# A hybrid decoder step on one core: values of the forgetting attention in a tile a head, the normalisation of a pair of heads taken up within the next pair, lasting zero-padded tiles for small inverses

## The chip, the core and the metric

The kernel runs on one core of a Trainium2 chip, as one launch. The time is the device time of that core in microseconds (us). The core has TensorE (PE), which does the matmuls and the transposes, VectorE (DVE), ScalarE (ACT), GpSimd (POOL), and SyncE (SP), whose queue issues most of the loads. Each engine takes its instructions in the order in which they were built in, and waits at the head of its queue for what that instruction needs. DMAs are issued from SP, ACT and POOL.

## The reference

One inference step with 1024 prompt tokens and 32 sample tokens. One input projection feeds four groups of heads; their outputs, each times a SiLU gate, are joined by an output projection and a layer norm. Two groups matter here:

```python
# C: forgetting attention (FoX), 8 heads x 64, blocks of 128 queries
s = einsum('bqhd,bkhd->bhqk', q, k) * 64 ** -0.5 + cq[.., :, None] - ck[.., None, :]   # cumulative log-forget
p = softmax(where(k_pos <= q_pos, s, -1e30));  o = einsum('bhqk,bkhd->bqhd', p, v)      # then times silu(c_gate)

# A: gated DeltaNet (GDN), 4 heads x 128, chunk-wise WY form, state S carried from chunk to chunk
sol = triangular_solve(eye + a, concat([v * beta, k * beta * exp(gam)]))               # per chunk
u = w_val - w_key @ S;  o = q_dec @ S + qk @ u;  S = S * chunk_dec + k_tail.T @ u
```

## The kernel before

The program runs in three stretches. First come the input projections, woven with the decoding of the sample tokens against the paged cache. The second, which the change touches, computes FoX and GDN for the prompt, woven with the last gate projections and with the cross-attention; the third does the SSD group, the output projection and the layer norm.

FoX takes its eight heads in pairs: `fox(hp)` does pair `hp`, heads `2*hp` and `2*hp + 1` (`h2` is 0 or 1). A head has four steps (`m`), each for two blocks of 128 queries. In a step PE computes logits into PSUM (`fs`, L588), DVE adds the forget term and takes the minimum (L592), ACT takes the exponential (L598), PE transposes the probabilities (`ft`), ACT or DVE copies them out (`P`), PE multiplies them with the values (`fo`, L620, whose weights are the tile `vt`), and DVE multiplies the result with the gate into `g2` (L626). The values of a pair are written to DRAM by `fox_v` in the first stretch as `vD[hp]`, 128 x 1024, and loaded into the one buffer of `vt` on SP's queue (L568), 512 KB. When both heads of a pair are done, the pair is normalised at once: DVE inverts the sums, ACT spreads them into `rr` (L636), PE transposes `rr` into the PSUM buffer that `ft` also uses (there is one), DVE multiplies into `g2` (L640), twice (`a`), and ACT's queue stores `g2`.

GDN takes 8 half-heads of four chunks (`i`). `gdn_solve` inverts the triangular matrices of half-head `i + 1` while `gdn_scan` carries the state through half-head `i`. The 16 x 16 inverses lie in DRAM (`dX`); `gdn_inv` clears a tile `D1` on DVE (L1039) and loads eight blocks into it (L1041, `D<-dX` in the trace). The matrices `A` have one buffer: the load for the next solve (L1057, `A<-aD`) waits until PE has done `l2p` (L1123), the last matmuls that read the old one. DVE reads the new one in `AL` (L1082).

The order on each engine is not written out by hand. Generators are woven (64 steps of FoX to 37 of GDN), and when the program is built a scheduler with a timeline of its own orders the instructions of each engine.

Of the kernel before, what the change touches and what calls it, by code (L numbers as in the profile page):

```python
# [21 lines left out]
T = 1024  # L22
# [148 lines left out]
class K:  # L171
# [356 lines left out]
    def fox_v(self, hp):  # L528
        nc, O = self.nc, self.O
        v = self.row_tile("vf")  # L530
        yield from self.projt(f"cv{hp}", lambda j, o, ps: self.copy(v[:, o:o + JW], ps))
        nc.scalar.dma_start(O["vT"][:, hp, :], v[:, :TT])
        vt = self.row_tile("vt")
        for a in range(2):
            p = self.g("vt")
            for b in range(4):
                n = 4 * a + b
                self.tr(p[:, b * 128:(b + 1) * 128], v[:, n * 128:(n + 1) * 128])
            self.copy(vt[:, 512 * a:512 * a + 512], p)
        nc.scalar.dma_start(self.vD[hp], vt[:, :T])  # L540
        p = self.g("vs")
        self.tr(p[:NS, 0:128], v[:, T:TT])
        nc.vector.tensor_copy(self.vs[:, hp * 128:(hp + 1) * 128], p[:NS, 0:128])

    def fox(self, hp):


        nc, fx = self.nc, self.fx
        vt = fx.tile([128, 8, 128], F32, tag="vt", name="vt", bufs=1)
        g2 = fx.tile([128, T], F32, tag="g2", name="g2", bufs=2)  # L550
# [5 lines left out]
        for h2 in range(2):  # L556
# [8 lines left out]
            self.marks.append(self.row(12 + hd, cB, nc.gpsimd))  # L565
            if h2 == 0:
                with behind(self.gl, hd - GL):
                    nc.sync.dma_start(vt, self.vD[hp].rearrange("p (n c) -> p n c", c=128))  # L568
                    nc.sync.dma_start(g2, self.gateD[8 + hp])
# [4 lines left out]
            for m in range(4):  # L574
                pair = (2 * m, 2 * m + 1)
                mns, Ss = {}, {}
                for qt in pair:
# [18 lines left out]
                    for i, (c0, c1) in enumerate(ch):  # L596
                        S, w = Ss[qt, i], c1 - c0
                        nc.scalar.activation(out=S[:, :w], in_=S[:, :w], func=AF.Exp, scale=-1.0, bias=mn[:, 0:1], accum_out=rs[:, qt, h2, i:i + 1])  # L598
                yield
                o = self.g("fo")  # L600
                for i in range(len(ch)):
# [11 lines left out]
                    for b4 in range(nb[pair[1]]):  # L613
                        kt = 4 * i + b4
                        for half in (1, 0):
                            qt = pair[half]
                            if b4 >= nb[qt]:
                                continue
                            with self.tc.issue_after(first.ins) if first else nullcontext():
                                d = nc.tensor.matmul(o[64 * half:64 * half + 64, 0:128], lhsT=vt[:, kt, 64 * h2:64 * h2 + 64],  # L620
                                                     rhs=P[qt, b4], start=(kt == 0), stop=(kt == qt), tile_position=(0, 64 * half))
                            first = first or d
                r = slice(64 * h2, 64 * h2 + 64)
                for half, qt in enumerate(pair):
                    s = slice(qt * 128, qt * 128 + 128)
                    nc.vector.tensor_tensor(out=g2[r, s], in0=o[64 * half:64 * half + 64, 0:128], in1=g2[r, s], op=ALU.mult)  # L626
                yield

        ri = fx.tile([128, 8, 2], F32, tag="ri", name="ri", bufs=2)
        nc.vector.tensor_tensor(out=ri, in0=rs[:, :, :, 0], in1=rs[:, :, :, 1], op=ALU.add)  # L630
        nc.vector.tensor_scalar(out=ri, in0=ri, scalar1=2.0, scalar2=None, op0=ALU.mult)
        nc.vector.reciprocal(ri, ri)
        for a in range(2):
# [6 lines left out]
            nc.vector.tensor_tensor(out=g2[:, s], in0=p, in1=g2[:, s], op=ALU.mult)  # L640
        nc.scalar.dma_start(self.mixD[2][:, hp, :], g2)

# [372 lines left out]
    def gdn(self):  # L1015


        w = {}

        self.scan = self.g("su")  # L1020
        self.gdn_inv(0)
        run(self.gdn_solve(0, w))
        self.gdn_loads(0)
        for i in range(8):
            nxt = {}
            solve = self.gdn_solve(i + 1, nxt) if i < 7 else iter(())
            for n, _ in enumerate(self.gdn_scan(i, w)):
                next(solve, None), next(solve, None)
                if n == 1 and i < 7:
                    self.gdn_loads(i + 1)  # L1030
                yield
            run(solve)
            w = nxt

    def gdn_inv(self, i):

        nc, (h, a), N = self.nc, divmod(i, 2), 4
        D1 = self.ga.tile([128, N, 32], F32, tag="D1", name="D1", bufs=2)
        nc.vector.memset(D1, 0.0)  # L1039
        for b in range(8):  # L1040
# [19 lines left out]
    def gdn_solve(self, i, w):  # L1060
# [13 lines left out]

        D1, DT1, AL, P1, P3 = self.D1[i], sm("DT1"), sm("AL"), sm("P1", 16), sm("P3")
        A, DT = big("A", D["A"], eng), big("DT")
        nc.vector.memset(DT, 0.0)
        if i < 7:
            self.gdn_inv(i + 1)
        nc.vector.transpose(out=fl(DT1), in_=fl(D1))  # L1080
        for q in Q:
# [8 lines left out]
        for n in range(N):  # L1090
            for i, q in enumerate(Q):
                nc.tensor.matmul(p[q, n * 16:(n + 1) * 16], lhsT=D1[q, n, :], rhs=P1[q, n, :], start=True, stop=True, tile_position=(32 * i, 32 * i))
        nc.vector.tensor_tensor(out=DT1[:, :, 16:32], in0=DT1[:, :, 16:32], in1=p[:, 0:N * 16].rearrange("p (n c) -> p n c", n=N), op=ALU.subtract)
# [542 lines left out]
    def run(self):  # L1636
# [4 lines left out]
        with ExitStack() as self.ctx_x:  # L1641
# [50 lines left out]

            def foxes():
                for hp in range(4):
                    yield from self.fox(hp)

# [112 lines left out]
```

## Time and profile before

| | |
|---|---|
| median of 3 runs | 1435.81 us (1434.82 to 1438.54) |
| the profiled execution | 1434.86 us, of which 1433.1 from its first to its last instruction |
| PE busy | 1329.7 us, 93% |
| DVE, ACT, POOL busy | 57%, 35%, 31% |
| granted TensorE clock, mean | 0.976 |

PE is nearly always busy, so what counts is when it stands still, what ended each such gap, and where its clock is below 1.00. Time in which another engine is idle counts only where PE waits behind it.

### The profile page before, as it was taken

To read this page: it belongs to the slowest core of one execution; us is meant where nothing else is said; L and a number is where in the kernel's file an instruction comes from. 1 tells how busy PE (TensorE), PEld (TensorE's weight loads), DVE (VectorE), ACT (ScalarE), POOL (GpSimd) and SP (SyncE) were. 2 spreads that over 40 slices of the span, in tenths; PEclk is the share of its full clock that TensorE was granted. 3 is DMA by queue.
4 is the path that set the end of the run, shared out by engine and by line. 5 is a ranking of instruction groups with operands and counts; after the bars stand their busy time and mean duration, and the time that the engine had idled before them with its cause. 6 is when DMAs were issued, how large, how long until landed. Compare 5 with 4: busy or idle time off the path is not lost. (4 is left out here: it accounts for less than half of the span.)

```text
span 1433.1 us, 30270 instructions
## 1 busy us (share of the span) xinstructions
PE 1329.7 (93%) x11222; PEld 1110.0 (77%) x11222; DVE 823.8 (57%) x2141; ACT 494.7 (35%) x1280; POOL 442.4 (31%) x465
## 2 busy tenths in 40 slices
PE   7999999999899999999998899898988979999995
PEld 6899888888778877888887878776766756666764
DVE  4523223256576767534245655677676648856588
ACT  4422222233435343322233244454444421213232
POOL 1445322233425444432212100011111026544456
PEclk9999999999999999999999999899999999999998
DMA  6559888978778897888877834657547576655322
GB/s 246 196 169 374 331 299 323 321 269 281 240 284 306 282 307 248 303 287 323 308 259 175 239 91 118 239 147 208 137 129 252 175 234 205 198 160 121 96 67 106
DMA packets 184477, 324.30 MB, mean 226 GB/s; under 512 B 47177, under 2 KB 110954, under 8 KB 184330
## 3 DMA queue, kind: packets, MB, share of 16 engines
q1 hardware_dynamic: 113744, 241.39, 50.4%
q10 hardware_dynamic: 41930, 59.11, 11.6%
q0 software_dynamic: 28656, 21.88, 6.2%
q8 instruction: 88, 1.44, 0.4%
q14 instruction: 59, 0.48, 0.1%
HBM read 262.23 MB, written 60.01 MB: 225 GB/s over the span
## 5 line engine op out<-in xcount | busy, mean ns | idle before, releaser
L356 PE MATMUL pj<-xh,wh 128*128 128x352 f32 x1152 | 382.2, 333 | 13.1 <-ACT wh L341 5.0
L356 PE MATMUL pj<-xh,wl 128*128 128x352 f32 x1152 | 379.5, 329 | 3.3 <-DVE wl L342 3.3
L356 PE MATMUL pj<-xl,wh 128*128 128x352 f32 x1152 | 379.1, 329 | 0.0
L356 PEld LDWEIGHTS pj<-xh,wh 128*128 128x128 f32 x1152 | 219.1, 191 | 28.1 <-issue 10.7
L356 PEld LDWEIGHTS pj<-xh,wl 128*128 128x128 f32 x1152 | 219.8, 191 | 11.5 <-issue 6.3
L356 PEld LDWEIGHTS pj<-xl,wh 128*128 128x128 f32 x1152 | 219.3, 190 | 10.6 <-issue 9.9
L1574 PE MATMUL op<-wo,mh 128*128 128x512 f32 x512 | 162.9, 398 | 3.1 <-DVE lr L1587 1.6
L672 POOL DMA_INDIRECT lf<-in_logf,ix x64 | 67.9, 1062 | 203.4 <-DVE cb L675 163.4
L342 POOL TENSOR_TENSOR wl<-wr,wh 128x1024 fp32r<-128x1024 f32 x41 | 97.9, 2387 | 104.3 <-ACT wh L341 94.3
L742 DVE SCALAR_TENSOR_TENSOR Oacc<-Oacc,dmb,dO 128x512 f32<-128x512 f32 x64 | 47.5, 743 | 142.3 <-PE dO L737 134.1
L1574 PEld LDWEIGHTS op<-wo,mh 128*128 128x128 f32 x512 | 95.6, 190 | 29.6 <-issue 6.0
L1574 PE MATMUL op<-wo,ml 128*128 128x512 f32 x256 | 102.0, 401 | 5.5 <-POOL ml L1546 5.5
L917 DVE SCALAR_TENSOR_TENSOR y<-u,cw,y 128x1080 f32<-128x1080 f32 x54 | 80.1, 1484 | 21.9 <-ACT y L915 21.5
L718 PEld LDWEIGHTS dA<-pg,QD 128*32 128x32 f32 x2048 | 59.8, 109 | 39.7 <-issue 25.8
L718 PE MATMUL dA<-pg,QD 128*32 128x128 f32 x2048 | 80.6, 275 | 7.6 <-DMA pg<-in_cache 7.5
L598 ACT ACTIVATE S<-S,mn 128x512 f32<-128x512 f32 (+2 forms) x96 | 58.5, 610 | 50.8 <-DVE mn L592 24.3
L737 PE MATMUL dO<-pg,dP 128*32 128x512 f32 x512 | 71.8, 605 | 4.1 <-ACT dP L734 3.9
L726 ACT ACTIVATE dmb<-dmb 128x1 f32<-128x1 f32 x64 | 18.7, 293 | 131.6 <-DVE dmb L725 116.3
L1574 PEld LDWEIGHTS op<-wo,ml 128*128 128x128 f32 x256 | 48.4, 189 | 20.2 <-POOL ml L1546 7.1
L592 DVE CUSTOM_DVE_ANT_0 S<-fs,cB 128x512 f32<-128x512 f32 (+2 forms) x96 | 52.5, 551 | 19.9 <-PE ft L219 15.0
L1193 POOL TENSOR_TENSOR rb<-ra,constG 128x4 f32<-128x4 f32 (+1 forms) x9 | 8.7, 971 | 156.5 <-DVE ra L1192 156.5
L620 PE MATMUL fo<-P,vt 128*64 128x128 f32 x576 | 47.9, 288 | 9.6 <-DMA vt<-vD 7.7
(521 smaller groups left out, 2450.2 us busy)
## 6 DMA issues: line engine op xcount, KB each, us to landing
pg<-in_cache SPq DMA_DIRECT2D x256, 512.0 KB
wr<-in_w_in SPq DMA_DIRECT2D x48, 512.0 KB
k<-kD POOLq DMA_DIRECT2D x16, 512.0 KB, 18.2
wq<-in_w_out SPq DMA_DIRECT2D x16, 512.0 KB
mr<-mixD SPq DMA_DIRECT2D x32, 256.0 KB
xr<-in_xT SPq DMA_DIRECT2D x8, 528.0 KB
gateD<-gt ACTq DMA_DIRECT2D x24, 176.0 KB
mrow<-in_w_mem SPq DMA_DIRECT2D x8, 512.0 KB
```

The costliest lines, as they stand in the source:

```text
L342: (eng or self.se).tensor_tensor(out=l, in0=r, in1=h.bitcast(F32), op=ALU.subtract)
L356: nc.tensor.matmul(ps[:n], lhsT=w[:, k, :], rhs=x[:, k, s], start=(k == 0 and q == 0), stop=(k == KD - 1 and q == 2))
L592: nc.vector.tensor_tensor_reduce(out=S[:, :w], in0=p[:, :w], in1=cB[:, c0:c1], op0=ALU.add, op1=ALU.min, scale=1.0, scalar=3e38, accum_out ...
L598: nc.scalar.activation(out=S[:, :w], in_=S[:, :w], func=AF.Exp, scale=-1.0, bias=mn[:, 0:1], accum_out=rs[:, qt, h2, i:i + 1])
L620: d = nc.tensor.matmul(o[64 * half:64 * half + 64, 0:128], lhsT=vt[:, kt, 64 * h2:64 * h2 + 64], rhs=P[qt, b4], start=(kt == 0), stop=(kt ...
L672: nc.gpsimd.indirect_dma_start(out=lf, out_offset=None, in_=I["logf"], in_offset=bass.IndirectOffsetOnAxis(ap=ix[:, j:j + 1].bitcast(U32), ...
L718: nc.tensor.matmul(ps[32 * b:32 * b + 32, 0:n], lhsT=QD[:, 4 * gr + b, hp, :], rhs=key(hp, b), start=(hp == 0), stop=(hp == 3), tile_posit ...
L726: nc.scalar.activation(out=mb[:, 1:2], in_=m, func=AF.Exp, scale=-1.0, bias=mb[:, 0:1])
L737: nc.tensor.matmul(po[32 * b:32 * b + 32, :], lhsT=P[:n, 32 * b:32 * b + 32], rhs=value(b), start=True, stop=True, tile_position=(0, 32 * b))
L742: nc.vector.scalar_tensor_tensor(out=O_, in0=O_, scalar=mb[:, 1:2], in1=po, op0=ALU.mult, op1=ALU.add)
L917: nc.vector.scalar_tensor_tensor(out=y, in0=u[:, i:i + CWD], scalar=w[:, i:i + 1], in1=y, op0=ALU.mult, op1=ALU.add)
L1574: nc.tensor.matmul(p[:m], lhsT=l[:, k, :], rhs=W[k][0][:, w, s], start=(k == 0 and q == 0), stop=(k == kn - 1 and q == 2))
```

## The change

- `fox_v` writes the values of a pair to DRAM as two halves, one a head. `fox` loads 256 KB for each head into a tile `vt` of its own, of which there are two; eight loads in place of four.
- The normalisation becomes a generator `fox_norm`. The next pair's `fox` takes it up in two parts: after the logits of its steps `m = 0` and `m = 1`, ahead of the products with the values. The last pair's runs at the end.
- Two tiles `D1z` are cleared once, and the loads of the 16 x 16 inverses write into them by turns, always at the same places. The refined inverse goes to a tile of its own instead of back into the loaded one.

```diff
         vt = self.row_tile("vt")
+        vv = vt[:, :T].rearrange("p (h n c) -> p n h c", h=2, c=64)
...
-            self.copy(vt[:, 512 * a:512 * a + 512], p)
+            self.copy(vv[:, 4 * a:4 * a + 4], p.rearrange("p (n h c) -> p n h c", h=2, c=64))
...
-    def fox(self, hp):
+    def fox(self, hp, ended):
...
-        vt = fx.tile([128, 8, 128], F32, tag="vt", name="vt", bufs=1)
...
-            if h2 == 0:
-                with behind(self.gl, hd - GL):
-                    nc.sync.dma_start(vt, self.vD[hp].rearrange("p (n c) -> p n c", c=128))
+            vt = fx.tile([128, 8, 64], F32, tag="vt", name="vt", bufs=2)
+            with behind(self.gl, hd - GL):
+                nc.sync.dma_start(vt, self.vD[hp][:, 512 * h2:512 * h2 + 512].rearrange("p (n c) -> p n c", c=64))
+                if h2 == 0:
                     nc.sync.dma_start(g2, self.gateD[8 + hp])
...
                 yield
+                next(ended, None)
                 o = self.g("fo")
...
-                                d = nc.tensor.matmul(o[64 * half:64 * half + 64, 0:128], lhsT=vt[:, kt, 64 * h2:64 * h2 + 64],
+                                d = nc.tensor.matmul(o[64 * half:64 * half + 64, 0:128], lhsT=vt[:, kt, :],
...
-
+        return self.fox_norm(hp, g2, rs)
+
+    def fox_norm(self, hp, g2, rs):
...
-        nc.scalar.dma_start(self.mixD[2][:, hp, :], g2)
+            if a == 1:
+                nc.scalar.dma_start(self.mixD[2][:, hp, :], g2)
+            yield
...
+        self.D1z = [self.ga.tile([128, 4, 32], F32, name=f"D1z{i}") for i in range(2)]
+        for t in self.D1z:
+            nc.vector.memset(t, 0.0)
...
-        D1 = self.ga.tile([128, N, 32], F32, tag="D1", name="D1", bufs=2)
-        nc.vector.memset(D1, 0.0)
+        D1 = self.D1z[i % 2]
...
-        D1, DT1, AL, P1, P3 = self.D1[i], sm("DT1"), sm("AL"), sm("P1", 16), sm("P3")
+        D0, D1, DT1, AL, P1, P3 = self.D1[i], sm("D1"), sm("DT1"), sm("AL"), sm("P1", 16), sm("P3")
...
-        nc.vector.transpose(out=fl(DT1), in_=fl(D1))
+        nc.vector.transpose(out=fl(DT1), in_=fl(D0))
...
             def foxes():
+                ended = iter(())
                 for hp in range(4):
-                    yield from self.fox(hp)
+                    ended = yield from self.fox(hp, ended)
+                run(ended)
```

The order on the engines is the same before and after as far as the second stretch, and there, and in a few places of the third, it is dealt anew. Three places, with the line numbers of each program:

SP's queue where the values of the third pair of heads are loaded (`vD_81`). Before:

```order
L1057 DMA Kp<-aD2Kp 128x512
L809 DMA dq<-dqD_86 128x1024
L1051 DMA g_12226<-gateD_125 128x512
L568 DMA vt<-vD_81 128x1024
L1041 DMA D_12851<-dX_122 16x4x16 x5
L1057 DMA A<-aD2A 128x512
```

After, the load for that pair's first head:

```order
L819 DMA dq<-dqD_85 128x1024
L1064 DMA g_11853<-gateD_125 128x512
L570 DMA vt<-vD_81 128x512
L572 DMA g_13185<-gateD_130 128x1024
L1054 DMA D1z_11227<-dX_121 16x4x16 x8
L1070 DMA A<-aD2A 128x512
```

It now stands twelve rows further up the queue than before, one solve earlier; the load for the second head of the pair stands where the one load stood.

DVE around `AL` of the third solve (`u` is what the scan's next matmuls on PE read, `P` the probabilities for `fo`). Before:

```order
L342 TENSOR_TENSOR wl<-wr,wh 128x1024
L1174 COPY wv<-su 128x128
L592 ISA S,mn<-fs,cB 128x128
L592 ISA mn 128x1
L1082 TENSOR_TENSOR AL<-A,constG 32x128 x4
L1161 TENSOR_TENSOR u<-wv,su 128x128
L216 COPY P<-ft 128x512
```

After:

```order
L342 TENSOR_TENSOR wl<-wr,wh 128x1024
L1174 TENSOR_TENSOR u<-wv,su 128x128
L216 COPY P<-ft 128x512
L595 ISA S,mn<-fs,cB 128x384
L595 ISA mn 128x1
L1095 TENSOR_TENSOR AL<-A,constG 32x128 x4
L1112 MEMSET D_11776 64x256
```

`u` and `P` moved from behind `AL` to ahead of it.

PE where the third pair of heads ends and the fourth begins (`fr` are the two transposes of the normalisation, `ft` uses the same PSUM buffer). Before:

```order
L620 MATMUL fo<-P,vt 64x128 x7
L219 MATMUL fr<-constG,rr 128x128 x4
L588 MATMUL fs<-k_14054,q_14053 128x512
L589 MATMUL fs<-k_14055,q_14053 128x512
L591 LDWEIGHTS identb
L591 MATMUL fs<-foxm,identb 128x128
L1139 MATMUL wv<-Vp,DT 128x128 x4
L219 MATMUL fr<-constG,rr 128x128 x4
```

After:

```order
L624 MATMUL fo<-P,vt 64x128 x7
L219 MATMUL fr<-constG,rr 128x128 x4
L1152 MATMUL wv<-Vp,DT 128x128 x4
L591 MATMUL fs<-k_14034,q_14033 128x512
L592 MATMUL fs<-k_14035,q_14033 128x512
L219 MATMUL ft<-constG,S 128x128 x3
```

After the same work PE comes to `ft` of the next pair instead of the second `fr`; that second `fr` stands seven rows further on.

## Rows read from the trace of the kernel before

**Rows 1.** Busy time by stretch: stretch, its length, each engine; clock, DMA share, GB/s.

```profile
800.00:1160.00 360.00, 327.15 (x3281) 264.65 (x3281) 237.94 (x763) 159.98 (x488) 38.30 (x52) 0.96 0.57 175
```

**Rows 2.** PE's waits, 800 to 1160 us: us in total, times, longest.

```profile
PE fo L620 <- DMA vt<-vD: 7.7, 1, 7.7
PE fr L219 <- DVE g L640: 6.5, 2, 5.0
PE l2p L1123 <- ACT DT L1118: 3.0, 1, 3.0
PE su L1164 <- DVE u L1161: 2.7, 1, 2.7
...
PE fs L588 <- DVE mn L592: 1.3, 1, 1.3
```

**Rows 3.** Timeline around that load: start, duration, what; idle before it.

```profile
993.01 0.41 SPq L568 DMA_DIRECT2D vt<-vD  x1
996.27 0.19 PE L1116 MATMUL lt<-D,P 32*32 32x32 f32 x1
1004.17 1.09 PE L620 MATMUL fo<-P,vt 128*64 128x128 f32 x6 [7.71 <-DMA vt<-vD]
```

**Rows 4.** Busy time by stretches of 10 us; the granted clock is third from the end.

```profile
900.00:910.00 10.00, 9.95 (x65) 8.68 (x66) 5.55 (x16) 2.13 (x8) 1.04 (x1) 0.83 0.57 177
...
1000.00:1010.00 10.00, 5.83 (x25) 4.87 (x26) 2.78 (x7) 1.02 (x4) 0.00 (x0) 0.53 0.10 35
1010.00:1020.00 10.00, 10.00 (x87) 8.87 (x87) 7.56 (x27) 5.61 (x18) 0.00 (x0) 1.00 0.45 139
```

**Rows 5.** Timeline of PE: the same four matmuls before and after the wait.

```profile
980.59 1.03 PE L819 MATMUL cs<-mk,dq 128*128 128x256 f32 x4
...
1005.88 1.91 PE L819 MATMUL cs<-mk,dq 128*128 128x256 f32 x4
```

**Rows 6.** Timeline of the loads of A and of what waits behind them.

```profile
891.70 0.37 SPq L1057 DMA_DIRECT2D A<-aD1A  x1
898.51 1.17 DVE L1082 TENSOR_TENSOR AL<-A,constG 32x128 f32<-32x128 f32 x4 [7.40 <-DMA A<-aD1A]
900.05 0.78 PE L1164 MATMUL su<-u,Kt 128*128 128x128 f32 x2 [2.67 <-DVE u L1161]
...
1010.65 0.34 SPq L1057 DMA_DIRECT2D A<-aD2A  x1
1013.26 1.17 DVE L1082 TENSOR_TENSOR AL<-A,constG 32x128 f32<-32x128 f32 x4 [1.39 <-DMA A<-aD2A]
...
1036.38 8.74 SPq L1041 DMA_DIRECT2D D<-dX  x7
1045.23 1.27 SPq L1057 DMA_DIRECT2D A<-aD3A  x1
...
1048.71 1.17 DVE L1082 TENSOR_TENSOR AL<-A,constG 32x128 f32<-32x128 f32 x4 [3.08 <-DMA A<-aD3A]
...
1079.27 0.32 SPq L1057 DMA_DIRECT2D A<-aD3A  x1
1086.25 1.17 DVE L1082 TENSOR_TENSOR AL<-A,constG 32x128 f32<-32x128 f32 x4 [4.07 <-DMA A<-aD3A]
1089.90 1.11 PE L219 MATMUL fr<-constG,rr 128*128 128x128 f32 x4 [5.02 <-DVE g L640]
```

**Rows 7.** SP's longest wait in all, and DVE's clearing of D1: ns min/median/max.

```profile
SPq L1041 <- DVE D L1039: 45.9, 4, 16.5
...
L1039 DVE MEMSET D<- x8: 165/165/165, 807.1 to 1036.2; 128x128 f32 x8
```

**Rows 8.** Timeline of SP's loads after the last load of A, and the first use of Kt.

```profile
1080.77 0.32 SPq L1057 DMA_DIRECT2D Kt<-aD3Kt  x1
1085.52 0.60 SPq L1544 DMA_DIRECT2D mr<-mixD  x1
1094.57 0.49 PE L1164 MATMUL su<-u,Kt 128*128 128x128 f32 x2
```

More of the change, by code (lines that the diff above doesn't have):

```diff
@@ L627, in fox @@
                 yield
+        return self.fox_norm(hp, g2, rs)
+    def fox_norm(self, hp, g2, rs):
+        nc, fx = self.nc, self.fx
         ri = fx.tile([128, 8, 2], F32, tag="ri", name="ri", bufs=2)
@@ L1015, in gdn @@
     def gdn(self):
-        w = {}
+        nc, w = self.nc, {}
         self.scan = self.g("su")
+        self.D1z = [self.ga.tile([128, 4, 32], F32, name=f"D1z{i}") for i in range(2)]
+        for t in self.D1z:
+            nc.vector.memset(t, 0.0)
         self.gdn_inv(0)
@@ L1091, in gdn_solve @@
             for i, q in enumerate(Q):
-                nc.tensor.matmul(p[q, n * 16:(n + 1) * 16], lhsT=D1[q, n, :], rhs=P1[q, n, :], start=True, stop=True, tile_position=(32 * i, 32 * i))
+                nc.tensor.matmul(p[q, n * 16:(n + 1) * 16], lhsT=D0[q, n, :], rhs=P1[q, n, :], start=True, stop=True, tile_position=(32 * i, 32 * i))
         nc.vector.tensor_tensor(out=DT1[:, :, 16:32], in0=DT1[:, :, 16:32], in1=p[:, 0:N * 16].rearrange("p (n c) -> p n c", n=N), op=ALU.subtract)
```

## The prediction

> **What bounds the kernel now.** I read the page first: PE is busy 93% of the span, so the other engines matter only where PE stands still behind them. The busy time by stretch then says where to look: in the second stretch, 800 to 1160 us, PE is busy 327.15 of 360 us, with DVE at 238 and ACT at 160 [rows 1]. So 33 us are open to this change, and nothing else there is near its limit. The list of PE's waits in that stretch names them [rows 2]: one wait of 7.7 us for the load of `vt`, 6.5 us in two waits before the transposes of the normalisation, 3.0 us behind ACT, 2.7 us behind DVE's `u`, 1.3 us behind DVE's logits. The reader should see that the first is a single event behind a DMA, and ask of each other whether the engine it names was itself waiting.
>
> The timeline answers for the first: the load of the third pair's values is issued at 993.01, after the last product of the pair before has freed the one buffer; PE's last matmul before the gap starts at 996.27, and the first product begins at 1004.17, 11.2 us after the issue [rows 3]. For two of the others the engine named was not the cause. At 900.05 PE had waited 2.67 us for `u`, but `u` stood on DVE behind `AL`, and DVE had waited 7.40 us for the load of A; at 1089.90 PE had waited 5.02 us for `g`, and DVE, ahead of that `g`, 4.07 us for A [rows 6]. The normalisation itself was hardly at fault.
>
> **The change part by part**, in us against the profiled execution's own 1434.86, which lies 0.95 under the median.
>
> *Values in a tile a head.* The third pair's first load stands one solve earlier on SP's queue, behind the gate load of that half-head, and its buffer was freed by the first head of the pair before, not by the second. A solve is some 34 us there, the distance of the loads of A at 1010.65, 1045.23 and 1079.27 [rows 6], so it goes out near 959; landing took 11.2 us for 512 KB [rows 3], and half of that is loaded, so it is there long before 996.3. The load for a pair's second head stands where the old one stood, a whole head ahead of its use. The wait of 7.71 goes: **-7.7**. Next after the products come transposes and the cross-attention, which followed the gap without a wait.
>
> *The clock behind that gap.* The granted clock is 0.53 of 2.4 GHz over 1000 to 1010 and 1.00 in the next ten [rows 4]. At two levels, 1.2 and 2.4 GHz, 0.53 means (1 - 0.53) x 10 / 0.5 = 9.4 us at the lower one, to about 1009.4. PE had stood idle before. The same four cross-attention matmuls took 1.91 there against 1.03 at full clock [rows 5]. PE worked 1009.4 - 1004.2 = 5.2 us at half clock, worth 2.6; DVE and ACT had little queued then. I take **-2.5**, ends 0 and -2.6.
>
> *Eight loads for four.* Four more issues on SP, at 0.41 each as that of rows 3, are 1.6 us of a queue that mostly waits [rows 7]; the cover is that each load is wanted much later. Cost 0, up to +1. Here a rule speaks against the change. The Trainium skill, "DMA: Bandwidth & Descriptors", section "Rules for kernel authors", wants a megabyte or more in a DMA for bandwidth, and these go from 512 to 256 KB. From that page's measured table (0.95 us for 64 KB, 6.15 for 1 MB) an estimate by a straight line is 3.3 us for one of 512 KB and 2 x 2.0 for two halves, 0.7 more a pair and 2.8 in all; if none of it were hidden the sum would shrink by 2.8. No run here shows such a split yet; the trace has only 2.6 to 7.0 us for a single 256 KB load [rows 6].
>
> *The copies in `fox_v`* keep their number, eight, and their elements, and write in runs of 64, in the first stretch and beside projections. No row shows the new form: 0, and at worst +1, a tenth of a microsecond each.
>
> *Two cleared tiles.* Six clears of 0.165 on DVE go, 1.0 us off PE's path: 0, ends 0 and -1. SP no longer waits for them (45.9 us, four times, [rows 7]). What stood behind it matters: before the seventh solve's A, seven loads of the small blocks held SP from 1036.38 for 8.74 us, and A went out at 1045.23 [rows 6]. After, the small loads wait for nothing late and A follows `l2p`. DVE's 3.08 for it can then go, and with it the 1.3 of PE behind it [rows 2]; other loads may still hold SP, so half: **-0.7**, ends 0 and -1.3.
>
> *The normalisation and the new order.* The waits for `fr` are 6.5, of which 5.02 is the last pair's [rows 2, 6]. There `ft` of the new pair now stands where the second `fr` stood, in the same PSUM buffer, and the evacuation it waits for still stands behind `AL` on DVE. The load of A still starts after `l2p`. The wait changes its name, not its size: 0, ends -5.0 and +1. At the third solve the order does help: `u` and `P` now stand ahead of `AL`, so PE can go on while DVE waits for A. Its 2.67 could go whole, and the clock of 0.83 over 900 to 910 [rows 4] adds (0.17 x 10 / 0.5) / 2 = 1.7. But DVE's backlog behind `AL` still comes out somewhere; I take half of the wait and no clock, **-1.3**, ends 0 and -4.4. The 3.0 behind ACT lies among casts of output weights, which move to later places; ends -3 and +3, taken as 0. At the fourth pair a load of `mr`, which waited until 1085.52, moves ahead of Kt. Kt would go out near 1086.1 instead of 1080.77; with 7.0, the longest landing of A, it is there at 1093.1, and wanted at 1094.57 [rows 6, 8]: 0, up to +2.
>
> Sum: -7.7 - 2.5 - 0.7 - 1.3 = **-12.2**, so 1422.7 for an execution like the profiled one, and 1435.81 - 12.2 = 1423.6 against the median. The third stretch starts when the second is done, and its loads are issued in turn by the same queues, so what is gained should arrive at the end.
>
> **The rivals.**
> 1. *The wait for A takes up part of the gain.* The load that landed in 2.6 us (1010.65 to 1013.26) followed the long gap, with DMA share 0.10 [rows 4]. Without the gap it may take the 7.0 us of 1079.27, 4.4 more on DVE. The Trainium skill, "DMA: Bandwidth & Descriptors", section "Issuing engines are not separate DMA queues", says that DMAs of all queues share the same engines; by that rule the trace agrees, 2.6 us in the quiet stretch. With one or two such waits 4 to 8 come back: 1428 to 1432. For: A still has one buffer. Against: no small loads queue ahead of it.
> 2. *Slower.* The new order lets DVE come to `AL` sooner, and more solves block it. So far four waits are shown, of 7.40, 1.39, 3.08 and 4.07, and PE lost 2.67 + 1.3 + 5.02 = 9.0 behind the three larger ones (14.55), 0.62 of each [rows 2, 6]. A new wait of 7.4 would cost 4.6. 2.7 of these eat the gain; from 3.6 the kernel is slower by over 0.3%; four give 1423.6 + 18.4 = 1442. Against: the order puts `AL` no nearer to `l2p` than before at the solves that I compared.
> 3. *The change doesn't do what it says.* The load of the third pair is held on SP behind the gate load, and lands as late as before. It would have to be held for over 25 us, against the longest wait of 16.5 in the list [rows 7]. Then only 2 come: 1434.
> 4. *More goes than summed:* the third solve's 4.4 whole, and part of the 5.0 and 3.0: 1414 to 1418.
>
> **How the numbers follow.** Chances: the forecast, 1418 to 1428, 0.57; rival 1, 0.20; rival 2, 0.11; rival 3, 0.04; rival 4, 0.08. About 0.3%, 4.3 us, is what a measurement of this kernel can tell from no change: faster means under 1431.5, slower over 1440.1. Faster: 0.57 + 0.08 + half of rival 1, 0.75. Slower: rival 2 from 3.6 waits on, 0.08. The rest, 0.17, is the same. The range that holds 8 in 10 runs from 1415, the sum with the third solve's ends and some of the 5.0, to 1436, which takes in rivals 1 and 3 and leaves rival 2 out.
>
> **What would show each step.** In the trace after, PE's wait for `vt` is gone and no stretch of ten us around the third pair's start has a clock near 0.53; SP shows no wait of `D1z` loads for DVE; a wait for `ft` behind DVE's `g` of some 5 us stands at the last pair; at the third solve PE's 2.67 is smaller. If DVE's waits for A add up to much over 16 us, rival 1 or 2 is at work. I am wrong if the wait for `vt` is still there, or if it is gone and PE's waits in the second stretch add up to as much as before.

## The result, and the profile after

The changed kernel takes 1445.36 us, median of 20 runs (1439.18 to 1456.81); the kernel before takes 1436.65 in 20 runs (1426.10 to 1449.90). The ratio is 1.0071, 95% interval 1.0048 to 1.0094: slower by 0.7%. The prediction said 1423.6, with a range of 1415 to 1436, and gave "slower" 0.08. Its profiled execution took 1448.70 us, with a span of 1446.9.

The page of the changed kernel, its first line and the busy time (share of the span, instructions) of PE:

```profile
span 1446.9 us, 30276 instructions
...
PE 1347.7 (93%) x11222; PEld 1121.8 (78%) x11222; DVE 823.9 (57%) x2135; ACT 495.8 (34%) x1280; POOL 443.9 (31%) x465
```

PE's idle time went down, from 1433.1 - 1329.7 = 103.4 us to 1446.9 - 1347.7 = 99.2. Its busy time went up by 18.0 us on the same 11222 matmuls. So the loss isn't in waits; the same work was done at a lower granted clock.

PE's waits in the second stretch, 800 to 1160 us (us in total, times, longest), which answer to [rows 2]; then the stretch's busy time, which answers to [rows 1], and the load for the third pair's first head on SP with the first product that uses it, which answer to [rows 3]:

```profile
PE ft L219 <- DVE g L648: 6.0, 2, 5.6
PE pj L356 <- DVE wl L342: 3.6, 3, 2.8
PE l2p L1136 <- ACT DT L1131: 3.5, 2, 2.2
PE pj L356 <- ACT wh L341: 2.4, 3, 1.5
PE fo L624 <- issue: 2.3, 1, 2.3
```

```profile
800.00:1160.00 360.00, 333.85 (x3303) 268.72 (x3297) 242.56 (x764) 162.53 (x491) 38.27 (x52) 0.97 0.62 179
```

```profile
967.63 0.88 SPq L570 DMA_DIRECT2D vt<-vD  x1
...
1000.88 0.44 PE L624 MATMUL fo<-P,vt 128*64 128x128 f32 x4
```

The wait for `vt` is gone: the load goes out 33 us ahead of its use. The wait for `fr` now bears the name `ft` and is as long. `u` no longer appears. So the second stretch did much of what was forecast. To find the loss I measure the stretches: the first ends at the first `AL`, the second at the end of the last `l2p`. Those two lines of the changed kernel (duration min/median/max in ns, first and last start):

```profile
L1095 DVE TENSOR_TENSOR AL<-A,constG x32: 270/282/289, 816.2 to 1087.5; 32x128 f32<-32x128 f32 x32
L1136 PE MATMUL l2p<-DT,A x64: 218/218/267, 868.4 to 1110.1; 64*64 64x64 f32 x64
```

The first stretch ended 7.8 us later than before (816.2 against 808.4), the second took 294.1 us in place of 300.3, and the last took 336.6 in place of 324.3. Gain 6.2, losses 7.8 and 12.3. PE's busy time in the second stretch and in the last (PE first, the clock third from the end), before and then after:

```profile
808.45:1108.76 300.31, 272.00 (x2739) 222.30 (x2738) 199.33 (x615) 137.84 (x423) 32.80 (x42) 0.95 0.57 170
1108.76:1433.10 324.34, 290.19 (x1890) 212.13 (x1889) 221.96 (x513) 87.00 (x164) 140.62 (x134) 0.97 0.50 152
```

```profile
816.21:1110.31 294.10, 273.73 (x2764) 223.43 (x2767) 199.88 (x615) 137.82 (x422) 33.08 (x43) 0.97 0.61 177
1110.31:1446.90 336.59, 302.32 (x1868) 217.20 (x1867) 220.80 (x508) 87.86 (x164) 140.28 (x134) 0.94 0.48 145
```

PE stood idle for 28.3 us of the second stretch before and 20.4 after, so 7.9 us of stops are gone. In the last stretch it stood idle for 34.2 and 34.3: the stops there are the same, and the 12.3 us are busy time at a lower clock. (In the changed kernel 25 more of PE's instructions stand ahead of the last `l2p`, some 3 us of work, so the two lengths don't cut at quite the same place.)

In the last stretch the code is the same in both kernels, but its 2069 instructions were dealt out anew, and not in a few places only, as I had it: row by row, over 420 of the 1436 matmuls of that code stand elsewhere in PE's order. Busy time there by stretches of 10 us (DVE, ACT, POOL behind PE and PEld; the granted clock is third from the end), the changed kernel first, then the kernel before:

```profile
1210.00:1220.00 10.00, 8.69 (x32) 3.81 (x32) 3.09 (x5) 0.00 (x0) 5.45 (x6) 0.51 0.47 162
1220.00:1230.00 10.00, 10.00 (x30) 5.82 (x29) 7.66 (x17) 2.94 (x4) 2.47 (x4) 0.63 0.52 110
```

```profile
1210.00:1220.00 10.00, 10.00 (x35) 5.79 (x34) 8.60 (x20) 3.20 (x5) 1.79 (x2) 1.00 0.60 137
1220.00:1230.00 10.00, 10.00 (x56) 7.57 (x55) 8.21 (x26) 0.89 (x2) 7.61 (x9) 1.00 0.76 263
```

PE is "busy" in both, but at 0.51 and 0.63 of 2.4 GHz, near its lower level of 1.2, in the changed kernel. What stands ahead of that, on POOL, in the changed kernel and then in the one before (start, duration, what, idle before it):

```profile
1193.69 1.28 POOL L1559 TENSOR_TENSOR ml<-mr,mh 128x512 fp32r<-128x512 f32 x1 [4.33 <-ACT mh L1558]
1200.26 0.63 POOL L1368 COPY Cz<-bx 64x128 f32<-64x128 f32 x2 [5.29 <-DMA bx<-bD]
1200.98 7.53 POOL L1307 TENSOR_TENSOR xS<-xS,cdS 128x1024 f32<-128x1024 f32 x4
...
1209.98 2.50 POOL L1395 TENSOR_TENSOR bE<-bE,cb 128x512 f32<-128x512 f32 x2
```

```profile
1193.78 8.52 POOL L1294 TENSOR_TENSOR xS<-xS,cdS 128x1024 f32<-128x1024 f32 x4 [3.27 <-PE xo L1281]
...
1203.77 2.51 POOL L1382 TENSOR_TENSOR bE<-bE,cb 128x512 f32<-128x512 f32 x2
1206.20 0.66 POOL L1355 COPY Cz<-bx 64x128 f32<-64x128 f32 x2
```

Before, the two copies `Cz` stood behind `bE`. After, they stand ahead of `xS`, wait 5.29 us for their load, and push `xS` and `bE` back. PE, which needs `bE`, stops there in the changed kernel:

```profile
1208.25 0.73 PE L1587 MATMUL op<-wo,mh 128*128 128x512 f32 x2
1211.31 1.12 PE L1402 MATMUL by<-bE,xdt 128*64 128x128 f32 x8 [2.33 <-POOL bE L1395]
```

The same eight matmuls took 0.66 us in the kernel before, 1.12 here.

### The profile page after: what moved, and what is told of

Its sections match the earlier page's. It is cut to its first block, busy times and chain, and to the rows that moved or that the text cites. A ratio compares the mean times of both kernels' runs of the same rounds, so it can differ in the third digit from the quotient of the medians.

```text
span 1446.9 us, 30276 instructions
## 1 busy us (share of the span) xinstructions
PE 1347.7 (93%) x11222; PEld 1121.8 (78%) x11222; DVE 823.9 (57%) x2135; ACT 495.8 (34%) x1280; POOL 443.9 (31%) x465
## 4 chain that ended last, share of the span: by engine, by line
PE 66%; DMA 14%; DVE 9%; issue 4%; ACT 3%; POOL 3%; SPq 0%; ACTq 0%; DVEq 0%; POOLq 0%
PE pj L356 29%; PE op L1587 9%; DMA pg<-in_cache 4%; PE dA L728 3%; PE dO L747 3%; PE fo L624 2%; DMA ggB<-gS 2%; PE ft L219 2%; PE i L320 2%; DVE y L927 1%; PE fs L591 1%; DMA bE<-gS 1%; PE fs L592 1%; PE co L844 1%; DVE gW L1019 1%
## 5 line engine op out<-in xcount | busy, mean ns | idle before, releaser
L1587 PE MATMUL op<-wo,mh 128*128 128x512 f32 x512 | 166.9, 407 | 3.0 <-DVE lr L1600 1.6
L1587 PE MATMUL op<-wo,ml 128*128 128x512 f32 x256 | 103.4, 406 | 2.0 <-POOL ml L1559 2.0
L1559 POOL TENSOR_TENSOR ml<-mr,mh 128x512 fp32r<-128x512 f32 x32 | 44.5, 1395 | 45.2 <-ACT mh L1558 44.8
L376 DVE SCALAR_TENSOR_TENSOR gt<-gt,pj 128x352 f32<-128x352 f32 (+1 forms) x48 | 24.3, 506 | 59.7 <-ACT gt L374 59.2
```

What stands on the lines that cost most here:

```text
L1559: nc.gpsimd.tensor_tensor(out=ml, in0=raw, in1=mh.bitcast(F32), op=ALU.subtract)
L1587: nc.tensor.matmul(p[:m], lhsT=l[:, k, :], rhs=W[k][0][:, w, s], start=(k == 0 and q == 0), stop=(k == kn - 1 and q == 2))
```

## The experiments

Theory A: the order dealt to the last stretch costs the time. Theory B: the new layout of the values holds up the first stretch. Theory C: the second stretch's gain is chance. Theory D, added on the way: the loads of A take back much of that gain. What became of C and D is told in the part on the prediction. One table for all runs; the lengths are of one profiled execution each. "Lost to clock" is PE's busy time x (1 - granted clock), summed over stretches of 5 us from 1110 us on: the time that the same work would have been shorter at full clock. "Both" runs from the first `AL` to the end; where the last `l2p` stands elsewhere among the other work (*), only that sum compares.

| kernel | ratio to before, 95% | second | last | both | lost to clock |
|---|---|---|---|---|---|
| before | 1 | 300.3 | 324.3 | 624.7 | 2.6 |
| after | 1.0071 [1.0048, 1.0094] | 294.1 | 336.6 | 630.7 | 15.4 |
| e5, after again | 1.0060 [1.0031, 1.0089] | 292.3 | 339.1 | 631.5 | 20.5 |
| e1, layout alone | 1.0010 [0.9974, 1.0045] | 300.9 | 324.1 | 625.0 | 4.4 |
| e8, values a head alone | 1.0009 [0.9974, 1.0045] | * | * | 624.7 | 7.9 |
| e2, without the split | 0.9996 [0.9964, 1.0028] | 297.9 | 327.6 | 625.6 | 7.2 |
| e3, split and lasting tiles | 1.0110 [1.0074, 1.0145] | 300.7 | 333.1 | 633.9 | 13.9 |
| e4, after, two copies moved | 1.0019 [0.9986, 1.0052] | 299.5 | 327.8 | 627.4 | 10.2 |
| e6, e4 and four state tiles | 0.9998 [0.9970, 1.0026] | 295.3 | 332.3 | 627.6 | 13.7 |
| e7, e2 with two tiles of A | 1.0013 [0.9976, 1.0049] | * | * | 623.5 | 12.2 |
| e9, stop filled with 10 | 1.0107 [1.0051, 1.0163] | 292.0 | 342.6 | 634.7 | 15.1 |
| e10, stop filled with 8 | 1.0050 [1.0015, 1.0085] | 292.4 | 335.8 | 628.2 | 11.0 |
| e11, split taken up later | 1.0026 [0.9994, 1.0058] | * | * | 628.9 | 11.9 |
| e12, stored in halves | 1.0113 [1.0069, 1.0157] | * | * | 634.1 | 8.3 |
| e13, after, order of before | 0.9965 [0.9928, 1.0003] | 293.7 | 324.6 | 618.2 | 6.0 |
| e15, e13 again | 0.9948 [0.9908, 0.9989] | 299.1 | 324.9 | 624.1 | 5.4 |
| e14, before, order of after | 1.0121 [1.0073, 1.0168] | 299.2 | 338.5 | 637.7 | 14.4 |
| e16, e13 with two tiles of A | 0.9903 [0.9873, 0.9934] | * | * | 610.3 | 7.5 |

**The parts, and the two copies.** e1 is the kernel before with the new layout:

```diff
-            self.copy(vt[:, 512 * a:512 * a + 512], p)
+            self.copy(vv[:, 4 * a:4 * a + 4], p.rearrange("p (n h c) -> p n h c", h=2, c=64))
...
-        vt = fx.tile([128, 8, 128], F32, tag="vt", name="vt", bufs=1)
+        vt = fx.tile([128, 2, 8, 64], F32, tag="vt", name="vt", bufs=1)
```

> The kernel before with one part of the change: the values are stored head by head, [h n c] in place of [n h c], and one tile a pair is still loaded at once. Every engine's order is that of the kernel before, row for row. Theory A (the order of the last stretch, which the change dealt anew, costs about 12 us, and the 7.8 us by which the first stretch ended later in the profiled execution are a difference from run to run): within 2 us of before, ratio 0.9985 to 1.0015. Theory B (the copies and the stores in the new layout hold up the first stretch): 6 to 8 us slower, ratio 1.004 to 1.006, and the first AL of the second stretch some 8 us later than 808.45.

No difference, and its two later stretches are those of before. Yet its first `AL` came at 814.62, late, though every engine has the order of the kernel before. The end of the first stretch lies anywhere from 804.9 to 820.8 us over these executions: a difference from one execution to the next. The interval of e1 still reaches 1.0045, so theory B falls in full only with e13 and e15 below, which have the new layout and aren't slower.

e2 leaves the split out of the change; against the changed kernel:

```diff
-                next(ended, None)
...
-        return self.fox_norm(hp, g2, rs)
-
-    def fox_norm(self, hp, g2, rs):
...
-            if a == 1:
-                nc.scalar.dma_start(self.mixD[2][:, hp, :], g2)
-            yield
+        nc.scalar.dma_start(self.mixD[2][:, hp, :], g2)
```

e3 keeps the split and the lasting tiles and leaves the values as they were:

```diff
-            self.copy(vv[:, 4 * a:4 * a + 4], p.rearrange("p (n h c) -> p n h c", h=2, c=64))
+            self.copy(vt[:, 512 * a:512 * a + 512], p)
...
-            vt = fx.tile([128, 8, 64], F32, tag="vt", name="vt", bufs=2)
+        vt = fx.tile([128, 8, 128], F32, tag="vt", name="vt", bufs=1)
```

> The changed kernel without one of its three parts: the normalisation of a pair stands again in one piece behind the pair; values in a tile a head and the lasting padded tiles stay. Its last stretch is dealt out as in the kernel before but for a few rows, its second has no load of values in front of a PV matmul. Theory A: the second stretch takes about 294 us as in the changed kernel (before 299.6), the last about 325 as before (changed 337), in sum 5 to 7 us faster than before, ratio 0.995 to 0.9965. Theory B: the 7.8 us of the first stretch stay, the 6 are won: 1 to 2 us slower, ratio 1.001. Theory C (the gain of the second stretch is itself chance): ratio 0.999 to 1.001 with both stretches as before.

> The kernel before with two of the three parts, the split normalisation and the lasting padded tiles; the values stay in one tile a pair, in the old layout, so the PV matmul can wait for their load. The last stretch is dealt out as in the changed kernel but for a few rows. Theory A: the last stretch takes about 337 us and nothing is won in the second, so 8 to 13 us slower than before, ratio 1.0055 to 1.009. Theory B: no new layout, so no loss in the first stretch: ratio 0.997 to 1.001.

e3 is slower, as theory A wanted, and by more than the 1.0055 to 1.009 expected: it has the order of the changed kernel's last stretch but for a few rows, and no new layout. e2 isn't slower, but the gain isn't there either: 0.9996 against the 0.995 to 0.9965 expected, which the interval hardly reaches. Its second stretch was only 2.4 us shorter, though PE's idle time there went from 28.3 to 22.5 us: PE waited 4.5 us for `P` of a small inverse, and the clock cost 3.5 us more than before.

e4 moves the two copies of the rows above, and nothing else on PE, ACT, POOL and SP:

```diff
-            for g in range(2):
-                nc.gpsimd.tensor_copy(cz[G[g], g, :], bx[G[g], 5, :])
+            with self.tc.issue_after(self.eB.ins) if n == 2 else nullcontext():
+                for g in range(2):
+                    nc.gpsimd.tensor_copy(cz[G[g], g, :], bx[G[g], 5, :])
```

> The changed kernel with two POOL copies of the last stretch (Cz of the third chunk of the SSD scan) moved from ahead of the four xS products to behind the bE products, as they stand in the kernel before; no other engine's order changes but for one DVE row. Theory A in its sharp form (these copies wait 5.3 us for their load, hold up xS and bE behind them, TensorE stops 2.3 us for bE and its granted clock then reads 0.51 and 0.63 for 20 us): the wait on bE of 2.3 us is gone, the clock there reads 1.00, and 2.3 + 20 x 0.43 = 10.9 us come back at most; I expect 6 to 10, so 1436 to 1439 us and a ratio to before of 1.000 to 1.003. Theory A in its broad form (many small losses all over the last stretch): 2 us come back, ratio 1.0055. Theory B: as the changed kernel, ratio 1.007.

About two thirds of the loss go by the ratios (1.0071 and 1.0060 against 1.0019, though the ends of the intervals overlap), and the stop at 1209 with them. The clock there (same columns as above):

```profile
1210.00:1220.00 10.00, 10.00 (x42) 5.27 (x39) 7.91 (x19) 2.42 (x4) 4.64 (x5) 0.83 0.59 195
1220.00:1230.00 10.00, 10.00 (x46) 7.18 (x45) 6.86 (x16) 2.54 (x5) 2.57 (x5) 1.00 0.87 262
1230.00:1240.00 10.00, 7.39 (x51) 3.85 (x49) 9.88 (x26) 3.25 (x4) 7.24 (x5) 0.76 0.45 151
```

0.51 and 0.63 became 0.83 and 1.00; the next stop, 2.6 us for the next `bE`, has the next low stretch.

**The same program, and the next wait.** e5 is the changed kernel again. e6 is e4 with four tiles for the states of the samples:

```diff
-            hs = sb.tile([128, 2, 256], F32, tag="shs", name="shs", bufs=2)
+            hs = sb.tile([128, 2, 256], F32, tag="shs", name="shs", bufs=4)
```

> The changed kernel once more, unaltered, for a second profiled execution. The lengths of the three stretches of one program vary: the program of before and the one with the layout alone ended the first stretch at 808.45 and 814.62 us. Theory A (the last stretch's order is the loss): from the last l2p to the end again 333 to 338 us, with the wait on bE of 2 us near 1210 and a granted clock well under 1.00 behind it. What the second stretch gains is open: 293.4 us in the first execution, but 298.9 in the kernel with the two copies moved, which has the same order there. If the gain is in the order, it is again 293 to 295; if the load of A takes most of it back, it is 296 to 299.

> The changed kernel with the two Cz copies behind bE, and with four tiles in place of two for the SSD states of the samples (shs), so that none of their four loads waits for a store. In the kernel with the copies moved the fourth is issued at 1272.87 us and TensorE waits 4.27 us for it, with a granted clock of 0.68 around it. Theory A: this wait and part of the clock go, 4 to 7 us against 1441, so 1434 to 1437 us, ratio to before 0.997 to 0.9995, and the last stretch takes 322 to 325 us. Rival: the later order of TensorE (products of the SSD chunks) sets the end, the wait goes elsewhere: 1439 to 1441 us, last stretch 327.

e5 repeats both the gain and the loss. In e6 the wait for `shs` is gone, but the time is e4's within the intervals, and the last stretch is no shorter: PE waits 3.6 us for a cast of `mr` and 3.1 for `sy` on DVE instead, and 5.3 for `bE` in place of 3.6. That is the rival.

**The second stretch.** e7 is e2 with another count of tiles:

```diff
-NBIG = dict(qd=2, QK=2, Kt=2, wv=2, wkT=2)
+NBIG = dict(A=2, qd=2, QK=2, Kt=2, wv=2)
```

e8 is the kernel before with the first part alone, the lines on `vt` and `vv` of the change's diff.

> The kernel without the split normalisation (values a head, lasting padded tiles), with two tiles for A, the operand of the small inverses, and one in place of two for wkT, so that the load of A can be issued a solve ahead. Tests whether the load of A takes back what the missing wait for the values gave: l2p of the fifth solve came 7 to 10 us earlier than in the kernels with one tile a pair (191.4 us behind the first AL against 198.3 to 201.9), of the eighth only 1 to 6 us. Theory D (A takes it back): VectorE's waits for A, 14 to 16 us in sum before, are under 3, the second stretch takes 288 to 293 us. Rival: the chain of small products between the solves sets the pace, or the one wkT tile costs as much: 295 us or more. The last stretch is dealt anew here, so the total says little of this.

> The kernel before with the first part of the change alone: values stored head by head and loaded into a tile a head. The wait of 7.7 us for the values goes. Theory of the prediction: second stretch 9 to 10 us shorter than 300. Theory D (the load of A takes most of it back): 2 to 5 us shorter, 295 to 298. The last stretch is dealt anew, differently from both kernels, so the total can lie on either side: ratio 0.994 to 1.006.

In e7 VectorE's waits for A are gone, and the seventh `l2p` comes 257.1 us behind the first `AL`, in e2 269.6; but it has another order than e2 in both later stretches, so neither that nor the total is A's alone. e8 doesn't tell: its eighth solve stands later among the other work. The wait for `vt` is gone there too, but a new one of 7.3 us for `P` stands ahead of `fo` (at 984.11), as long as the old one: with it, no gain shows.

**Filling the stop.** e9 and e10 add matmuls that nobody reads where PE waits for `bE`, ten and eight:

```diff
+            for _ in range(10 if n == 1 else 0):
+                with self.tc.issue_after(self.xsl.ins):
+                    nc.tensor.matmul(Y[0][:, 256:512], lhsT=self.c("ident"), rhs=bx[:, 0:2, :], start=True, stop=True)
```

> The changed kernel with ten more matmuls (128x256, about 0.3 us each, their result is not used) on TensorE at the place where it waited for bE near 1209 us, so that it is not idle there; POOL's order ahead of it is the changed kernel's (the Cz copies still hold up xS and bE). Two products of the output stand behind the SSD products now, and some rows of the rest are dealt anew. Theory A with the clock (the stop itself is cheap, 2 us, and what costs is that the granted clock reads 0.51 to 0.77 for the 20 us behind it): with the stop filled the clock stays above 0.9 there, 5 to 9 us come back although ten matmuls are added: 1438 to 1442 us, ratio to before 1.001 to 1.003, as with the copies moved. Rival (the clock falls there by itself, or by the kind of work behind the stop): no gain or 1 us slower than the changed kernel, ratio 1.006 to 1.008, clock about 0.6 at 1210 to 1230.

> The same with eight matmuls in place of ten: a second sample of the same question, since the clock differs from one execution to the next. Theory A with the clock: ratio 1.001 to 1.003 and a clock above 0.9 at 1210 to 1230. Rival: 1.006 to 1.008, clock about 0.6.

Both missed the time that I expected, and both have some other rows in another order too. In e10 the clock held, but the added work took 3.7 us, not the 2.4 that eight times 0.3 make, and the low stretch came later, at 1230 to 1250. In e9 the clock fell just before 1220, though since 1195 PE had made no stop of over 0.84 us. The stretch from 1220 us, e10 first, then e9:

```profile
1220.00:1230.00 10.00, 10.00 (x50) 7.45 (x50) 6.73 (x18) 2.58 (x4) 0.94 (x2) 1.00 0.70 222
```

```profile
1220.00:1230.00 10.00, 10.00 (x34) 4.30 (x32) 5.95 (x16) 2.80 (x4) 1.88 (x2) 0.50 0.55 173
```

So the stop at 1209 isn't alone the cause of the low clock, and what brings it down stays open.

**Other orders with the whole change.** e11 takes the split up behind the products with the values, e12 stores each half of the normalised rows when it is done. Both keep the computation and get other orders. e11, then e12:

```diff
-                next(ended, None)
                 o = self.g("fo")
...
+                next(ended, None)
                 r = slice(64 * h2, 64 * h2 + 64)
```

```diff
-            if a == 1:
-                nc.scalar.dma_start(self.mixD[2][:, hp, :], g2)
+            nc.scalar.dma_start(self.mixD[2][:, hp, s], g2[:, s])
```

> All three parts of the change, with the step of the split normalisation taken up one place later, behind the PV matmuls in place of ahead of them. The work is the changed kernel's; the last stretch is dealt out in a third way, in which the xS products stand behind bE on POOL and the fourth load of shs ahead of the third bE. Theory A (not a part of the change is slow, but the order that the last stretch got with it): the last stretch takes 323 to 331 us in place of 337 to 339, the second still 292 to 299, ratio to before 0.996 to 1.002. Rival (the split itself costs, by work or by its late store): 1.005 to 1.009 again, whatever the order.

> All three parts of the change, with the normalised rows stored in two halves, each when it is done, in place of in one piece. The work is the changed kernel's; the last stretch is dealt out in a fourth way, with the xS products far ahead of the SSD chunks on POOL. Theory A: last stretch 320 to 331 us, ratio to before 0.995 to 1.002. Rival (the split itself costs): 1.005 to 1.009.

The same work gave 1.0026 and 1.0113, outside the 0.996 to 1.002 and 0.995 to 1.002 expected, e11 only just. e11 speaks for theory A in its total, though its interval overlaps that of the changed kernel; e12's order is bad by itself: PE waited 9.2 us for `P` of the cross-attention and 7.1 for a copy of `wv` in the second stretch, and 5.1 for `xS` in the last. These two left the split under suspicion, since no kernel with it had the old order.

**The orders crossed.** e13 is the changed kernel with the last stretch held, engine by engine, in the order in which the kernel before was built; e14 is the kernel before with that of the changed one. The table lists the place of each instruction in the code; the edges set the order of issue and no wait:

```diff
+LAST = {
+    "SP": """
+0 3 6 9 12 15 37 42 1010 47 1040 52 57 62 67 72 102 111 120 129 138 147 156 165 179 225-228 24-25 471-473 520-522 1013 1043 1073 1103 1133 1163 1070
...
+    def replay(self, ins):
+        info = mybir.DependencyInfo(mybir.DependencyClass.NoSync, mybir.DependencyReason.DATA)
+        for row in LAST.values():
...
+            for i, j in zip(seq, seq[1:]):
+                self.tc.add_manual_dep(ins[j], ins[i].name, info, reason="order")
```

> The changed kernel, all three parts, with the instructions of the last stretch (2069 of them, from the loads of the first output weights on) held on each engine in the order in which the kernel before has them; the first and the second stretch are the changed kernel's. Theory A: the last stretch takes 324 to 328 us as in the kernel before, the second 292 to 299: 2 to 8 us faster than before, ratio 0.9945 to 0.999. Rival (the split or the values cost by themselves, in whatever order): ratio 1.004 to 1.009 as the changed kernel.

> The kernel before, without any part of the change, with the instructions of the last stretch held on each engine in the order in which the changed kernel has them; the first and the second stretch are those of the kernel before, with the wait of about 8 us for the values. Theory A: the last stretch takes 333 to 339 us, the second 300: 9 to 14 us slower than before, ratio 1.006 to 1.010. Rival (the parts of the change cost, not the order): ratio 0.998 to 1.002.

This settles the cause. With the old order all three parts are no longer slower: e13 is faster by its median, with an interval that just reaches 1.0003, and e15 below, the same kernel, is faster clear of 1. Without any part of the change, the new order alone is slower, by as much as in e3 and by more than the 1.006 to 1.010 expected. The added edges cost nothing that shows: the last stretch of e13 is as long as that of the kernel before, and that of e14 as long as those of the changed kernel. PE's waits in the last stretch, 1155 us to the end, of e13 and then of e14:

```profile
PE op L1630 <- POOL ml L1602: 2.8, 3, 1.7
PE op L1632 <- DVE accs L1591: 2.8, 1, 2.8
...
PE by L1445 <- POOL bE L1438: 1.0, 2, 0.6
```

```profile
PE by L1433 <- POOL bE L1426: 7.2, 4, 2.3
PE yi L1522 <- DMA shs<-in_sst: 3.9, 1, 3.9
PE op L1620 <- DVE accs L1579: 2.8, 1, 2.8
```

And the clock of e14, the low stretch of the changed kernel in a kernel with no part of it:

```profile
1210.00:1220.00 10.00, 7.68 (x39) 4.40 (x37) 4.43 (x7) 0.62 (x1) 10.00 (x9) 0.82 0.13 52
1220.00:1230.00 10.00, 10.00 (x30) 4.54 (x27) 4.68 (x12) 1.26 (x2) 2.38 (x3) 0.50 0.80 152
```

**A version that beats both.** e15 repeats e13; e16 is e13 with the two tiles of A of e7.

> The changed kernel with the last stretch in the order of the kernel before, once more, unaltered, for a narrower interval. If the first measurement holds: ratio 0.994 to 0.999, second stretch 292 to 296 us, last 324 to 327. If it was a lucky set: 0.999 to 1.002.

> The same with two tiles for A and one in place of two for wkT, so that the load of A is issued a solve ahead, and the last stretch still in the order of the kernel before. With two tiles alone VectorE's waits for A were gone and the seventh solve came 12.5 us earlier, but the total was 1.0013 with another order at the end. If the waits for A bound the second stretch: 3 to 8 us faster than the kernel without it, ratio 0.990 to 0.995. If the chain of products between the solves bounds it, or the one tile of wkT costs as much: 0.995 to 0.999, no difference.

e15 holds in its total, 1428.73 us; its profiled execution is the longest of the six, 1444.84, and its second stretch of 299.1 misses the 292 to 296 expected. e16 takes 1424.28 us, 1.0% under the kernel before. What ended VectorE's idle time at tile A (us, times), in the changed kernel and in e16:

```profile
  DMA A<-aD3A: 7.7, 2
  ACT DT L1131: 7.3, 4
  DMA A<-aD1A: 3.8, 1
  DMA A<-aD2A: 2.6, 2
```

```profile
  PE lp L1142: 3.7, 2
  issue: 1.8, 6
```

The 14.1 us of DMA waits are gone.

## Why the prediction was wrong

**The step that failed** is the last of the sum: "The third stretch starts when the second is done, and its loads are issued in turn by the same queues, so what is gained should arrive at the end." It gave the order of the last stretch no term at all. I had looked at where the change moved instructions in the second stretch, and took the moves behind it for a few. They cost 12.3 and 14.8 us in the two executions of the changed kernel, and e14 shows 14.2 without any part of the change. Most of that is clock: 5.1 us lost on average in the last stretch with the old order or nearly (before, e1, e2, e13, e15), 16 with the new one (after, e5, e3, e14). Two misplaced copies are part of it (e4); I could not divide the rest by cause, and why the clock falls more often in the new order stays open.

**The wait for the values (-7.7)** went, as forecast. In the kernels with one tile a pair it was 7.7 (before), 8.3 (e14), 8.7 (e1) and 5.1 us (e3); in the kernels with a tile a head no wait for `vt` shows. The fifth `l2p` came 188.3 to 194.6 us behind the first `AL` in the eight executions with the changed kernel's order there (after, e4, e5, e6, e9, e10, e13, e15), against 201.1 to 201.9 in before, e1 and e14.

**The copies and the loads (0).** e1 shows no cost of the new layout within its interval; the copies on DVE take 688 ns against 686. The rule of a megabyte or more (the Trainium skill, "DMA: Bandwidth & Descriptors", section "Rules for kernel authors") would have taken 2.8 back by my estimate. (The straight line gives 3.4 us for 512 KB, not 3.3, and so 2.4 back.) The trace shows no such loss: the 256 KB go out at 967.63 and are wanted at 1000.88, so all of it is hidden.

**The clock (-2.5)** was not won. At 1000 to 1010 us it does read 1.00 in the changed kernel, but in e13, with the same order there, 0.56. Lost to clock between 810 and 1110 us is 9.4, 9.1 and 8.8 us in before, e1 and e14, and from 4.7 (e5) to 15.4 (e15) in the eight: 9.2 on average. It only falls elsewhere.

**A behind the small loads (-0.7)** did not come. At the seventh solve the small loads were issued by 1038.2 and no longer held A, but a load of `g`, 512 KB, went out at 1040.60, ahead of A at 1041.94. `AL` started 5.6 us after that, where it took 3.5 before [rows 6], and DVE waited 3.68 us in place of 3.08; whether `g` slows A is not tested. PE, which had lost 1.35 us there, now lost 2.32. The profile puts that stop down to "issue", but it ended with `g` on DVE, which frees the buffer of `fo` and stood behind `AL`; in e3 the trace names `g` for the same stop:

```profile
1041.94 0.34 SPq L1070 DMA_DIRECT2D A<-aD3A  x1
1047.54 1.17 DVE L1095 TENSOR_TENSOR AL<-A,constG 32x128 f32<-32x128 f32 x4 [3.68 <-DMA A<-aD3A]
1048.72 0.29 DVE L630 TENSOR_TENSOR g<-fo,g 64x128 f32<-64x128 f32 x1
1049.11 0.62 PE L624 MATMUL fo<-P,vt 128*64 128x128 f32 x6 [2.32 <-issue]
```

**`u` and `P` ahead of `AL` (-1.3)** gave the larger end of its range without the clock: PE's 2.67 for `u` is gone whole. **The normalisation (0)** is right: `ft` waits 5.61 us at 1090.88 where `fr` waited 5.02.

**What the second stretch gave.** PE's idle time in it is 28.3, 28.4 and 27.9 us in before, e1 and e14, and 18.0 to 21.7 in the eight: 8.1 us of stops are gone on average, where the sum without its clock had 9.7. That is no chance, so theory C falls. In length the eight average 294.8 us and the three 300.1, so 5.3 won: no clock was won, and in six of the eight those 25 instructions more stand ahead of its end.

**Rival 1** has the right number for the change with its order held, 1429.16 and 1428.73 where it said 1428 to 1432, but not the mechanism. Its sign, DVE's waits for A at much over 16 us, isn't there: they are 14.1 us against 15.9 [rows 6]. The load that it had in mind took 2.6 us in the ten us with a DMA share of 0.45, not of 0.10 [rows 4], and without the gap 3.4 us, not up to 7.0:

```profile
1008.43 0.34 SPq L1070 DMA_DIRECT2D A<-aD2A  x1
1011.78 1.17 DVE L1095 TENSOR_TENSOR AL<-A,constG 32x128 f32<-32x128 f32 x4 [1.64 <-DMA A<-aD2A]
```

So theory D isn't shown. e16, without those waits, is 4 to 5 us faster than e13 and e15, but the intervals overlap, and it has one tile less of `wkT` and another order in the second stretch; how much the loads of A cost stays open.

**Rival 2** has the right sign and the wrong mechanism: VectorE's waits for A didn't grow.

## What to carry to other kernels

Where a scheduler deals out the order, an edit in one stretch can re-deal a later one whose code nobody touched: read the order to the end of the program, and give every re-dealt stretch a term with both signs. Before a change is judged, hold the untouched stretches in their old order, or run the new order without the change; here that turned 0.7% slower into 0.35 to 0.5% faster (the first of these not clear of no change), and opened the way to 1.0%. And look at busy time next to idle time: PE lost 18 us while its idle time shrank.

## What the runs showed of the hardware

- Low-clock stretches cost more than the stops that some of them follow: a stop of 2.33 us stood ahead of 20 us at 0.51 and 0.63, worth 8.7 x 0.49 + 10 x 0.37 = 8.0 us. In e9 such a stretch came without a stop of over 0.84 us shortly before it, and in the kernel before PE's busy share dropped to 7.77 of 10 us at 1270 with the clock at 1.00. A single stop doesn't tell whether the clock falls.
- Over the whole span, PE's busy time x (1 - granted clock) is 22 us in the profiled execution of the kernel before and 40 in that of the changed one, 1.6% and 2.8%. It grew by more than the whole loss of 13.8 between these two, since idle time fell by 4. The Trainium skill, "TensorE: Matmul & The Clock Gate", section "Part 1: The HAM clock gate (the "warmup" mystery)", puts the penalty of the ramp under 1% of a typical kernel's span; it says so of the warm-up, and the figures here count every fall in mid-program too, so they don't contradict it.
- The first stretch, with the same order on PE in each, ended anywhere between 804.9 and 820.8 us. Only stretches compare well between single executions; the totals want many.
